# A hybrid decoder layer on one core: the edges of the first feed-forward reordered, and the mixer's output stage fed through another queue

## The chip, the core and the metric

The kernel runs on one core of one Trainium2 chip. The metric is device time in microseconds (us) of one execution. TensorE (PE in the profile) multiplies, VectorE (DVE), ScalarE (ACT) and GpSimd (POOL) compute on tiles, and SyncE (SP) only issues transfers. Transfers can be issued from SP, ACT and POOL; each of these works its own instructions off in order, so an issue that has to wait holds up all that stands behind it.

## The reference

One layer, sequence length 1024, model width 1024, all in float32:

```python
f = swiglu(rmsnorm(h, g1), w_gu, w_down)          # silu(h@Wg) * (h@Wu) @ Wd, d_ff = 2816
h = h + 0.5 * rmsnorm(f, g1_post)
m = hybrid_mixer(rmsnorm(h, g_mix), ...)          # 16 stick-breaking attention heads beside a
h = h + rmsnorm(m, g_mix_post)                    #   Mamba-2 scan; concat(att, ssd) @ w_out (2048 x 1024)
c = memory_cross_attention(rmsnorm(h, g_xa), rmsnorm(mem, g_mem), ...)
h = h + rmsnorm(c, g_xa_post)
f = swiglu(rmsnorm(h, g2), w_gu2, w_down2)        # the second feed-forward
return h + 0.5 * rmsnorm(f, g2_post)
```

Inside the mixer the attention output and the two groups of the scan's output each pass a norm of their own before `w_out`.

## The kernel before, in words

**Layout.** Activations lie transposed: 8 tiles `d` of 128 features, in two halves `hh` of 512 tokens. Every float32 operand is split into two float32r parts, hi (a rounded copy, made on ACT) and lo (the rest, made on DVE). A product is three matmuls: hi·hi, hi·lo and lo·hi (`mm3`). `XH[hh][d]` and `XL[hh][d]` are the two parts of the current input; `XH` tiles have one fixed place each, the `XL` tiles of a half share nine places (`xl0`, `xl1`) that go to whoever asks next.

**Order.** TensorE's order is written out by hand. `self.clock` adds up what each matmul is planned to cost (0.216 us for 512 columns), and a list `later` holds pieces of work for the other engines, each with a planned time; `run_later` issues what has come due, pinned behind what its engine was given before. `run_later(T)` takes all that is due up to T at once. Work that is not pinned is ordered by a planner with its own estimates.

**The first feed-forward, up (`up_phase`).** The first 3 of 22 blocks are plain products with weights split on the fly. The other 19 use Strassen-like sevens: seven products of quarter size (12 matmuls each) instead of eight (`seven`). A seven needs sums of input quarters: `S1`, `S4`, `S5`, and `B21`, `B12`, which overwrite the parts of the input that the plain products used. `fetch` reads the quarters a, d, b, c again from memory (pairs "ad", "bc"); `below` makes `B21` from the pair "ca" while the second half's plain products run, and `last` makes `B12` from the pair "bd" once they are done (`again` loads it). Each first scales one tile of its pair on ACT, then makes the difference on DVE and splits it. Two "ca" pairs lie in `raw2`, which is also where raw weights land; the other "ca" and the "bd" pairs lie in `blk` (three places, shared with split weights). The weights' own sums (`wc`) are made on GpSimd. For the blocks computed before block 4 the sums of activations that the down product needs are made from a copy read back from memory (`act_sums`, four loads on GpSimd's queue, five sums on DVE, five stores on ACT's queue); for the others `pair_sums` makes them from tiles still at hand. At its end `up_phase` calls `run_later(self.clock + 4600)`.

**Weights prepared ahead (`prepare`, `prepare_all`).** While the sevens run, 37 weights of the mixer's input product are loaded in 74 halves (256 KB), split, and both parts stored to memory, so that later they are only loaded. Loads and stores go on SP's queue; 62 halves have planned times 4.3 us apart, the last 12 fall in the down product, 9 us apart.

**Down (`down1`, `down7`).** Seven products `m` = 0 to 6, each over 11 blocks `j` of 256 features, 132 matmuls each. `fetch` loads for each j the weight and the sum of activations, on SP's queue; two of the four weight quarters stay in tiles named by `stay`, 11 each, in places of the former input. Weight and activation parts go to the eight places `wp` and `dx`, and to `hl`. After each product `finish` plans what follows: squares for the norm, loads of the residual (`resid`, GpSimd's queue), and `post`, which scales by the norm, adds the residual, stores the new h, and takes the columns and rows of the next norm (`rms_cols`, `rms_rows`: small products on TensorE) at two times named `tail`.

**Mixer.** `ssd` and `attention` follow. During `attention` 8 of the 16 weights of `w_out` (those of the scan's half) are prepared in 16 halves, 20 us apart; the other 8 are loaded raw and split when used. A head's output is added into `mix_d` in memory by accumulating transfers on GpSimd's queue (`finish`). `mix_first` does the first pass (half 0, scan part), six of eight output tiles beside the end of attention, the last two in `mix_out`. `mix_out` then does three passes: (half 0, attention), (half 1, scan), (half 1, attention), 192 matmuls each, two output tiles at a time. `load(kt, hh)` reads a tile of `mix_d` on SP's queue into `oraw` (four places), adds its square to a sum, and splits it. Weights come through `wstream`, one ahead, three places for hi and lo each; raw ones through two `wraw`.

Of the kernel before, what the change touches and what calls it, by code (L numbers as in the profile page):

```python
# [10 lines left out]
F32 = mybir.dt.float32  # L11
# [32 lines left out]

NOSYNC = mybir.DependencyInfo(mybir.DependencyClass.NoSync, mybir.DependencyReason.DATA)


class Kern:
# [142 lines left out]
    def prepare(self, names, raw, pairs, times):  # L191
# [9 lines left out]

        def load(n):
            pool, tag, bufs = raw[n % len(raw)]
            raws[n] = self.t(pool, [P, 4, P], F32, tag, bufs=bufs)
            self.kp(nc.sync.dma_start(out=raws[n], in_=work[n][0][:, work[n][2], :]))
# [9 lines left out]
        def store(n):  # L215
            for d, x in zip(work[n][1], parts.pop(n)):
                self.kp(nc.sync.dma_start(out=d[:, work[n][2], :].bitcast(F32), in_=x.bitcast(F32)))
# [20 lines left out]
    def prepare_all(self, sp):  # L238
# [9 lines left out]
        self.prepare(names, raw, pairs, a[:k] + [420000 + 9000 * i for i in range(n - k)])  # L248
# [124 lines left out]
    def resid(self, hh, step, start=0):  # L373


        def one(d):
            self.XL[hh][d] = self.xl(hh, F32)
            self.kp(self.nc.gpsimd.dma_start(out=self.XL[hh][d], in_=self.h[hh][d]))
# [179 lines left out]
    def up_phase(self, sp, sp2, wgu, gpre, act_d, bank, load, plain, sizes, rw=None, begin=None):  # L558
# [39 lines left out]
        def act_sums(j, t0):  # L598

            x = {}  # L600
            names = ("a11", "a21", "a12", "a22")

# [22 lines left out]
            for i, (n, out, a, b, op) in enumerate((  # L625
# [4 lines left out]
                at(t0 + 9000 + 1200 * i, combine, n, out, a, b, op)  # L630
                at(t0 + 12000 + 1200 * i, put, n)
# [29 lines left out]
        def tiles(n, src):  # L661
            if n in early:
                tmp[n] = self.t(rw, [P, 2, H], F32, "raw2", bufs=2)
            else:
                tmp[n] = self.t(sp2, [P, 2, H], F32, "blk", bufs=NBLK)
            for i, (hh, d) in enumerate(src):
                self.kp(nc.gpsimd.dma_start(out=tmp[n][:, i], in_=self.h[hh][d]))
# [21 lines left out]
        def steps(k):  # L689
            a, d = (lambda i=i: tmp["ad", k][:, i] for i in range(2))  # L690
            b, c = (lambda i=i: tmp["bc", k][:, i] for i in range(2))
# [12 lines left out]
        def below(k):  # L704
            c, a = (tmp["ca", k][:, i] for i in range(2))
            scale(a, k)
# [5 lines left out]
        def last(k):  # L712
            b, d = (tmp["bd", k][:, i] for i in range(2))
            scale(d, k + 4)
# [116 lines left out]
        early = [("ad", k) for k in range(4)] + [("ca", k) for k in range(2)] if begin else []  # L831
# [17 lines left out]
        if begin:  # L849
# [40 lines left out]
        for k in range(4):  # L890
# [23 lines left out]
    def down1(self, sp, wdn, act_d, xs_d, gpost, gnext):  # L914
# [4 lines left out]
        stay = {(1, 1): L_[0][4:8] + H_[0][4:8] + H_[0][0:3], (0, 0): H_[1][4:8] + L_[1][4:8] + H_[1][0:3]}  # L919
# [10 lines left out]
        def finish(m, i):  # L930
# [5 lines left out]
            elif m == 4:  # L936
# [968 lines left out]
    def mix_out(self):  # L1905
# [3 lines left out]
        with self.pools("mo", ["r", "a"], ["b"]) as (rp, sp, sp2, dnp):  # L1909
# [15 lines left out]
            def load(kt, hh):  # L1925
                raw = self.t(sp, [P, H], F32, "oraw", bufs=4)
                nc.sync.dma_start(out=raw, in_=self.mix_d[kt][:, hh * H : (hh + 1) * H])
                if kt < 8:
                    square(kt, raw)
# [5 lines left out]
                self.scaled_split(hi, lo, raw, self.par("ssd_norm_g" if kt >= 8 else "attn_norm_g", kt % 8))  # L1935
                return hi, lo
# [405 lines left out]
```

## Time and profile before

| what | us |
|---|---|
| median of 3 runs (lowest to highest) | 2640.93 (2639.95 to 2643.17) |
| the profiled execution: time, span | 2636.82, 2635.0 |
| PE busy, share of the span | 2586.5, 98% |
| DVE, ACT, POOL busy | 1983.5, 1292.7, 579.3 |
| mean clock granted to TensorE | 0.995 of full |
| up product of the first feed-forward ends at | 454 |
| attention and the first pass's start end at | 1576 |

The span runs from the first to the last instruction, and the rest of the time lies around it. In a row of a windows table "x" is the number of instructions in the stretch and PEclk the granted clock; a stretch of TensorE is undisturbed when 50 us hold 222 matmuls of 512 columns. A row of waits names who waited, on what, the total in us, how often, and the longest. A row of a timeline has start and length in us, engine, line, operation, tiles, and in brackets the idle time before it and what ended it; SPq and POOL rows with DMA are issues, whose data land later.

### The profile page before, as it was taken

Reading aid. Unit: us, or ns where it says so; the run is one execution under the profiler, and the core shown is the slowest. Engines: PE = TensorE matmul, PEld = TensorE weight load, DVE = VectorE, ACT = ScalarE, POOL = GpSimd, SP = SyncE. Lnnn points to the kernel's source line nnn. Section 1 sums busy time; section 2 is a strip of 40 time slices with the busy share of each in tenths; the row PEclk is TensorE's granted clock in tenths of the full one; section 3 lists DMA queues with packets and bytes.
Section 4 is the critical chain, followed back from the end, with each engine's and each line's share of the span. In section 5 each row is a group of like instructions: output and inputs, shape, how many; then the busy total and the mean of one; then the engine's idle time right before and its main releaser. Section 6 shows DMA issues by size and latency. Waiting matters only on the chain.

```text
span 2635.0 us, 36828 instructions
## 1 busy us (share of the span) xinstructions
PE 2586.5 (98%) x12850; PEld 2153.3 (82%) x12850; DVE 1983.5 (75%) x3044; ACT 1292.7 (49%) x2300; POOL 579.3 (22%) x677
## 2 busy tenths in 40 slices
PE   9999999999999999999999999999999999999999
PEld 7788887878777778888888897888878788888887
DVE  6778887779679774777777777767556888777777
ACT  7434443555356563555555555345554433333553
POOL 2555553000100000111111110101011555452000
PEclk9999999999999999999999999999999999999999
DMA  5558888884654226645555556547558453226654
GB/s 208 183 187 287 276 272 285 283 278 154 243 184 168 81 73 199 177 142 150 141 157 132 167 153 225 187 150 250 197 184 296 140 176 116 99 98 227 188 170 154
DMA packets 215274, 489.82 MB, mean 186 GB/s; under 512 B 26544, under 2 KB 35120, under 8 KB 215088
## 3 DMA queue, kind: packets, MB, share of 16 engines
q1 hardware_dynamic: 168656, 381.02, 44.1%
q0 software_dynamic: 23104, 63.98, 8.1%
q10 hardware_dynamic: 23328, 42.48, 4.3%
q8 instruction: 101, 1.65, 0.3%
q14 instruction: 85, 0.70, 0.1%
HBM read 327.46 MB, written 138.94 MB: 177 GB/s over the span
## 4 chain that ended last, share of the span: by engine, by line
PE 83%; DVE 6%; DMA 5%; issue 3%; ACT 2%; POOL 1%; SPq 0%; DVEq 0%; POOLq 0%; ACTq 0%
PE mm L139 45%; PE dn L139 30%; PE z L139 2%; PE tr L142 2%; PE y L139 1%; PE ms L142 1%; PE ms L139 1%; DMA wraw<-in_w_dn 1%; PE seg L139 1%; DMA oraw<-mix 1%; DVE nb L1731 1%; DVE wlo L265 1%; PE st L139 0%; POOL wc L732 0%; DMA ev<-mix 0%
## 5 line engine op out<-in xcount | busy, mean ns | idle before, releaser
L139 PE MATMUL mm<-xh,whi 128*128 128x512 f32 x1320 | 520.5, 403 | 5.3 <-DVE xl L1899 2.3
L139 PE MATMUL mm<-xh,wlo 128*128 128x512 f32 x1272 | 489.1, 392 | 0.6 <-ACT xh L263 0.6
L139 PE MATMUL mm<-xl,whi 128*128 128x512 f32 (+1 forms) x1252 | 486.7, 389 | 1.5 <-DVE xl L265 1.2
L139 PEld LDWEIGHTS mm<-xh,whi 128*128 128x128 f32 x1320 | 248.3, 188 | 47.3 <-issue 3.8
L139 PEld LDWEIGHTS mm<-xh,wlo 128*128 128x128 f32 x1272 | 238.9, 188 | 53.0 <-ACT xh L263 1.0
L139 PEld LDWEIGHTS mm<-xl,whi 128*128 128x128 f32 x1252 | 236.2, 189 | 35.1 <-DVE xl L265 1.6
L1731 DVE TENSOR_TENSOR_SCAN nb<-nb,begin 128x128 f32<-128x128 f32 (+7 forms) x128 | 171.5, 1352 | 52.3 <-ACT nb L1727 51.4
L1727 ACT ACTIVATE nb<-z,scale 128x128 f32<-128x128 f32 (+2 forms) x192 | 107.9, 581 | 77.3 <-PE z L139 76.9
L265 DVE TENSOR_TENSOR wlo<-wraw,whi 128x1024 fp32r<-128x1024 f32 x70 | 85.4, 1221 | 54.2 <-ACT whi L263 53.9
L263 ACT CAST whi<-wraw 128x1024 fp32r<-128x1024 f32 (+1 forms) x87 | 83.8, 964 | 78.6 <-PE mm L139 54.2
L654 ACT ACTIVATE ft<-ft 128x512 f32<-128x512 f32 x88 | 55.5, 632 | 106.6 <-DVE ft L653 104.7
L1748 POOL DMA_DIRECT2D mix<-sq x64 | 52.8, 826 | 228.2 <-DVE sq L1746 168.2
L139 PE MATMUL dn<-xh,wlo 128*128 128x512 f32 x296 | 101.2, 390 | 1.3 <-DMA wlo<-dwlo 1.3
L732 POOL TENSOR_TENSOR wc<-wraw,raw 128x512 f32<-128x512 f32 x56 | 79.5, 1420 | 60.7 <-DVE whi L265 16.0
L732 POOL TENSOR_TENSOR wc<-raw,wraw 128x512 f32<-128x512 f32 x55 | 81.6, 1484 | 50.7 <-DVE blk L265 21.3
L265 DVE TENSOR_TENSOR atl<-tr,ath 128x512 fp32r<-128x512 f32 (+1 forms) x108 | 67.9, 631 | 29.9 <-ACT ath L263 29.6
L817 POOL TENSOR_TENSOR ft<-ft,e 128x512 f32<-128x512 f32 x37 | 60.0, 1622 | 121.2 <-DVE e L816 45.0
L263 ACT CAST ath<-tr 128x512 fp32r<-128x512 f32 (+1 forms) x108 | 58.9, 546 | 55.2 <-PE tr L142 50.9
L139 PE MATMUL mm<-ath,v 128*128 128x256 f32 x320 | 85.7, 290 | 0.3
L139 PE MATMUL dn<-xh,blk 128*128 128x512 f32 x264 | 85.2, 389 | 0.0
L263 ACT CAST wlo<-wc 128x512 fp32r<-128x512 f32 x79 | 49.1, 621 | 70.7 <-PE dn L139 23.7
L139 PE MATMUL mm<-atl,v 128*128 128x256 f32 x320 | 82.7, 281 | 0.7 <-DVE atl L265 0.7
(552 smaller groups left out, 6777.2 us busy)
## 6 DMA issues: line engine op xcount, KB each, us to landing
whi<-dwhi SPq DMA_DIRECT2D x82, 512.0 KB, 3.6
wlo<-dwlo SPq DMA_DIRECT2D x82, 512.0 KB, 4.7
wraw<-in_w_gu SPq DMA_DIRECT2D x43, 512.0 KB, 4.0
raw<-in_w_gu SPq DMA_DIRECT2D x37, 512.0 KB, 4.2
dwhi<-bh SPq DMA_DIRECT2D x70, 256.0 KB, 4.1
dwlo<-bl SPq DMA_DIRECT2D x70, 256.0 KB, 4.2
wraw<-xs SPq DMA_DIRECT2D x56, 256.0 KB, 3.1
xs<-ft ACTq DMA_DIRECT2D x54, 256.0 KB, 3.1
```

The lines of the kernel that those rows point to most:

```text
L139: self._pe(self.nc.tensor.matmul(out, lhsT, rhs, start=start, stop=stop, skip_group_check=self.more), cost)
L142: self._pe(self.nc.tensor.transpose(out, src, self.ident if ident is None else ident), 109.0)
L263: self.kp(self.nc.scalar.copy(hi, src))
L265: self.nc.vector.tensor_tensor(out=lo, in0=src, in1=hi.bitcast(F32), op=ALU.subtract)
L654: nc.scalar.activation(t, t, AF.Silu)
L732: nc.gpsimd.tensor_tensor(out=t, in0=a, in1=b, op=op)
L817: nc.gpsimd.tensor_tensor(out=t1, in0=t1, in1=e, op=ALU.mult)
L1727: nc.scalar.activation(nb[:, s0:s1], z[:, 0:n], AF.Sigmoid, scale=sc[:, i : i + 1])
L1731: nc.vector.tensor_tensor_scan(out=nb[:, 0:Wd][:, ::-1], data0=nb[:, 0:Wd][:, ::-1], data1=begin[:, S - Wd : S][:, ::-1], initial=0.0, op0 ...
L1748: nc.gpsimd.dma_start(out=self.mix_d[p][a * 64 : a * 64 + 64, csl], in_=o, accum_op=ALU.add)
```

## The change

Eight things change in the first feed-forward, and three in the mixer. The second feed-forward shares `up_phase` and keeps its path (`begin` is None there).

1. Three of the "ca" pairs and three of the "bd" pairs get places of their own (`homes`: `braw` twice, `rpost` and `dg`, `acc0` and `acc1`, which the preparation of weights uses only later); none lies in `raw2` any more, and of these pairs `blk` holds two instead of six. The first three "ca" loads are planned 13, 18.5 and 5 us earlier, the first three "bd" loads 9.5, 7 and 4.5 us earlier.
2. The scaling of a tile of the pair is taken out of `below` and `last` and planned on its own, before them.
3. `last` is planned every 1.2 us instead of 1.5.
4. `act_sums` makes its sums 14 us after its loads are planned instead of 9, and stores 3 us after that.
5. The call `run_later(self.clock + 4600)` at the end of `up_phase` is gone.
6. In `down1` the stay tiles of quarter (1, 1) are taken in another order: the first four are `XH[0][4:8]`, the next four `XL[0][4:8]`.
7. The last 12 halves of prepared weights are loaded and stored on GpSimd's queue (`switch`).
8. The columns and rows of the next norm of half 0 are planned at 17 and 20.5 us after the last tile instead of 11 and 16, and the first four squares of half 1 15 us later and closer together.
9. All 16 weights of `w_out` are prepared during attention, 32 halves, 12 us apart.
10. `mix_out` reads attention's tiles back on GpSimd's queue, into eight places of `oraw`, the eight of its first pass in one go, and squares them after the split.
11. The residual's loads in `mix_out` start later (16 us, then 3.5 us apart) and each waits for the TensorE instruction that was last issued when it was planned (`hold`).

```diff
-    def prepare(self, names, raw, pairs, times):
+    def prepare(self, names, raw, pairs, times, switch=float("inf")):
+        def queue(n):
+            return nc.sync if times[n] < switch else nc.gpsimd
...
-        self.prepare(names, raw, pairs, a[:k] + [420000 + 9000 * i for i in range(n - k)])
+        self.prepare(names, raw, pairs, a[:k] + [420000 + 9000 * i for i in range(n - k)], 418000)
...
+    def hold(self, inst):
+        self.tc.add_manual_dep(inst.ins, self.prev.name, SYNC, reason="not before this product")
...
+            late = 14000 if begin else 9000
-                at(t0 + 9000 + 1200 * i, combine, n, out, a, b, op)
-                at(t0 + 12000 + 1200 * i, put, n)
+                at(t0 + late + 1200 * i, combine, n, out, a, b, op)
+                at(t0 + late + 3000 + 1200 * i, put, n)
...
-        early = [("ad", k) for k in range(4)] + [("ca", k) for k in range(2)] if begin else []
+        early = [("ad", k) for k in range(4)] if begin else []
+        homes = {}
+        if begin:
+            for k, x in enumerate((
+                [(rw, "braw", 2)] * 2, [(rw, "rpost"), (self.tp, "dg")], [(rw, "acc0"), (rw, "acc1")],
+            )):
+                homes["ca", k] = homes["bd", k] = x
...
-            for k, t in enumerate((27000, 33500, 34000, 34500)):
+            for k, t in enumerate((14000, 15000, 29000, 34500)):
                 at(t0 + t, tiles, ("ca", k), [(0, k + 4), (0, k)])
+                at(t0 + 34000 + 1500 * k, lambda k=k: scale(tmp["ca", k][1], k))
...
-                            at(self.clock + 12500 + 500 * k, again, k)
+                            at(self.clock + 3000 + 3000 * k, again, k)
+                            at(self.clock + 12000 + 1000 * k, lambda k=k: scale(tmp["bd", k][1], k + 4))
...
-            at(self.clock + 1500 * k + (0 if begin else 500), last, k)
+                at(self.clock + 3500, lambda: scale(tmp["bd", 3][1], 7))
+            at(self.clock + (1200 * k if begin else 1500 * k + 500), last, k)
...
-        self.run_later(self.clock + 4600)
+        if not begin:
+            self.run_later(self.clock + 4600)
...
-        stay = {(1, 1): L_[0][4:8] + H_[0][4:8] + H_[0][0:3], (0, 0): H_[1][4:8] + L_[1][4:8] + H_[1][0:3]}
+        stay = {(1, 1): H_[0][4:8] + L_[0][4:8] + H_[0][0:3], (0, 0): H_[1][4:8] + L_[1][4:8] + H_[1][0:3]}
...
-                self.post(0, gpost, self.C[0], gnext, step=2600, accs=accs[:])
+                self.post(0, gpost, self.C[0], gnext, step=2600, accs=accs[:], tail=(17000, 20500))
-                    at(2000 + 4000 * d, squares, 1, d, "bh")
+                    at(17000 + 2500 * d, squares, 1, d, "bh")
...
-            self.prepare([("out", i) for i in range(8, 16)], *self.prep_pool(wsp), [self.clock + 30000 + 20000 * i for i in range(16)])
+            self.prepare([("out", i) for i in [*range(8, 16), *range(8)]], *self.prep_pool(wsp), [self.clock + 30000 + 12000 * i for i in range(32)])
...
+            def read(kt, hh):
+                raw = self.t(sp, [P, H], F32, "oraw", bufs=8)
+                nc.gpsimd.dma_start(out=raw, in_=self.mix_d[kt][:, hh * H : (hh + 1) * H])
+                return raw
...
-            for k in range(8):
-                prefetch(1, k)
-            self.resid(0, 5000, 12000)
+            raws = [read(k, 0) for k in range(8)]
+            acts[1] = [load(k, 0, raws[k]) for k in range(8)]
+            self.resid(0, 3500, 16000, True)
```

More of the change, by code (lines that the diff above doesn't have):

```diff
@@ L662, in tiles @@
             if n in early:
-                tmp[n] = self.t(rw, [P, 2, H], F32, "raw2", bufs=2)
-            else:
-                tmp[n] = self.t(sp2, [P, 2, H], F32, "blk", bufs=NBLK)
-            for i, (hh, d) in enumerate(src):
-                self.kp(nc.gpsimd.dma_start(out=tmp[n][:, i], in_=self.h[hh][d]))
+                t = self.t(rw, [P, 2, H], F32, "raw2", bufs=2)
+            elif n in homes:
+                t = [self.t(*x[0:1], [P, H], F32, *x[1:]) for x in homes[n]]
+            else:
+                t = self.t(sp2, [P, 2, H], F32, "blk", bufs=NBLK)
+            tmp[n] = t if isinstance(t, list) else [t[:, i] for i in range(2)]
+            for x, (hh, d) in zip(tmp[n], src):
+                self.kp(nc.gpsimd.dma_start(out=x, in_=self.h[hh][d]))
         def scale(x, d):
@@ L712, in last @@
         def last(k):
-            b, d = (tmp["bd", k][:, i] for i in range(2))
-            scale(d, k + 4)
+            b, d = tmp["bd", k]
+            if not begin:
+                scale(d, k + 4)
             combine(B12[k], b, k, d, ALU.subtract)
@@ L1923, in square, with load @@
                     nc.vector.tensor_tensor(out=asum[-1], in0=asum[-1], in1=sq, op=ALU.add)
[L1925 to L1929, printed above, removed]
+            def read(kt, hh):
+                raw = self.t(sp, [P, H], F32, "oraw", bufs=8)
+                nc.gpsimd.dma_start(out=raw, in_=self.mix_d[kt][:, hh * H : (hh + 1) * H])
+                return raw
+            def load(kt, hh, raw=None):
+                if raw is None:
+                    raw = read(kt, hh)
                 if kt < 8:
```

23 lines of the change are left out of this document (15 added, 8 removed).

## The prediction, made before the change was run

> **What bounds the kernel now.** I read the page first, then the waits of TensorE, then windows around each wait, then the timelines of the engines that caused it.
>
> ```profile
> span 2635.0 us, 36828 instructions
> PE 2586.5 (98%) x12850; PEld 2153.3 (82%) x12850; DVE 1983.5 (75%) x3044; ACT 1292.7 (49%) x2300; POOL 579.3 (22%) x677
> ```
>
> TensorE is the bound. No part of the change takes a matmul away, so all that can be won is time in which TensorE waits or runs at a lower clock. These are the waits in the stages that the change touches (who <- on what: us, times, longest).
>
> ```profile
> PE dn L139 <- ACT whi L998: 6.5, 1, 6.5
> PE mm L139 <- DVE xl L265: 2.6, 3, 1.2
> PE ms L139 <- DVE acc L365: 2.5, 2, 2.3
> PE mm L139 <- ACT xh L263: 2.4, 2, 1.8
> PE dn L139 <- ACT F L1050: 1.6, 1, 1.6
> PE dn L139 <- DVE olo L272: 1.5, 2, 0.8
> PE dn L139 <- DMA wlo<-dwlo: 1.3, 1, 1.3
> PE dn L139 <- DVE e L796: 0.8, 1, 0.8
> PE mm L139 <- DVE e L796: 0.7, 1, 0.7
> ```
>
> The last two rows are those of the stretch 75 to 150. A wait costs more than its length where the clock falls after it. The windows show it (us, PE busy with number of matmuls, the other engines, PEclk, DMA share, GB/s):
>
> ```profile
> 88.08:91.50 3.42, 3.42 (x9) 2.65 (x10) 2.95 (x5) 2.44 (x5) 1.46 (x3) 0.50 0.88 286
> 101.73:105.15 3.42, 3.42 (x10) 2.64 (x9) 3.42 (x6) 0.62 (x1) 2.19 (x2) 0.50 0.00 0
> 456.72:463.55 6.83, 3.22 (x8) 2.43 (x9) 5.80 (x9) 4.02 (x7) 1.32 (x3) 0.50 1.01 350
> 668.35:671.76 3.41, 3.41 (x10) 2.63 (x9) 3.41 (x7) 1.24 (x2) 0.54 (x1) 0.50 1.03 409
> 1596.77:1600.19 3.42, 3.38 (x8) 2.48 (x8) 3.42 (x5) 2.09 (x4) 0.00 (x0) 0.50 0.46 159
> 200.00:250.00 50.00, 50.00 (x222) 41.40 (x222) 42.42 (x61) 23.11 (x41) 28.24 (x19) 1.00 0.82 281
> 50.00:100.00 50.00, 46.20 (x193) 36.70 (x191) 40.66 (x53) 28.15 (x47) 23.87 (x32) 0.97 0.60 205
> 100.00:150.00 50.00, 47.32 (x200) 38.28 (x200) 35.41 (x52) 15.79 (x28) 30.76 (x27) 0.97 0.50 175
> 450.00:500.00 50.00, 43.53 (x186) 35.47 (x185) 40.96 (x66) 29.11 (x52) 3.19 (x4) 0.93 0.91 319
> ```
>
> 222 matmuls in 50 us make 0.225 us each and 15.2 in 3.42 us. So the five dips cost (15.2-9), (15.2-10), (14.3-8, in the 3.22 us that were busy), (15.2-10) and (15.2-8) matmuls: 1.4, 1.2, 1.4, 1.2 and 1.6 us. The counts bound the stages: 50 to 150 lacks 222-193 + 222-200 = 51 matmuls or 11.5 us, 450 to 500 lacks 36 or 8.1 us.
>
> **The change, part by part.**
>
> *Start of the sevens (homes, scaling apart, earlier loads).* Size: 2.6 + 2.4 of waits and 1.4 + 1.2 of dips, 7.6 us. What lies behind them, on GpSimd:
>
> ```profile
> 63.29 1.06 POOL L667 DMA_DIRECT2D raw<-in_xT  x2 [1.78 <-ACT S L263]
> 69.99 1.06 POOL L667 DMA_DIRECT2D raw<-in_xT  x2 [5.64 <-issue]
> 90.03 1.06 POOL L667 DMA_DIRECT2D blk<-in_xT  x2 [2.15 <-DVE bl L683]
> ```
>
> The "ca" pairs wait at 63 and 70 for `raw2` to be given up, and the last "bd" pair at 90 for `blk`. These places are the cause: the change gives the pairs others, empty until 152 of the planner's time. No instruction is added; four ACT scalings move ahead, still before their readers. The loads move past GpSimd's sums of weights, which at POOL's 24 to 31 us per 50 have room. B12 can only be written after the last plain product, and its fourth pair is still in `blk`: this may leave a rest. Bounds 0 and 10 (11.5 less the next 1.5). I take 7.
>
> *act_sums 5 us later.*
>
> ```profile
> 115.52 5.17 DMA dg<-act
> 120.16 1.29 DVE L616 TENSOR_TENSOR xl<-cb,cb 128x512 f32<-128x512 f32 x2 [3.93 <-DMA cb<-act]
> ```
>
> DVE stood 3.9 us for data that landed at about 120; 5 us later they are there. What DVE held up was e, for which TensorE waited 0.8 and 0.7. Now `cb`'s three places come free 5 us later, and `pair_sums` of block 5 needs them: DVE could stand there instead. Bounds -3.9 and 1.5; I take 1.4, as the planner knows that order.
>
> *Edge to the down product (stay order, no `run_later`, GpSimd's queue).*
>
> ```profile
> 435.54 5.32 SPq L984 DMA_DIRECT2D xh<-in_w_dn  x8
> 454.68 3.17 SPq L984 DMA_DIRECT2D xl<-in_w_dn  x4
> SPq L217 <- DVE bl L213: 3.0, 2, 1.9
> 454.68 4.95 DMA xl<-in_w_dn
> ```
>
> The first two are from SP's timeline, the third from its waits between 425 and 470, the last from the chain that ended last. The first down product starts with the stay tiles in `xl`, issued last, at 454.7, when the last seven's B11 frees them; the `xh` ones were issued at 435. With `xh` first, the four blocks that are needed first are there by 454. The `xl` ones are then needed from 454 + 4 x 2.7 = 465, and landed by about 463 (issued to 457.9, 4.95 to land), with their split still to come: little slack, so a rest may come back. Without `run_later` SP does not meet the stores of prepared halves that are due then before the first seven fetches; the activation stores that go later with them are read four blocks on, 10 us. Size: 6.5 + 1.4 = 7.9 (count: 8.1). Bounds 0 and 8.1; I take 6.8.
>
> [...] The sum above rests on the order of the stay tiles.
>
> Those halves cost GpSimd 36 issues at about 0.54 us each (the 1.06 of two above), 19 us on an engine that is busy 3.2 of 50 us there; SP no longer stands for their conversions. What this is worth is the wait for F, 1.6: bounds 0 and 1.6, I take 0.8.
>
> *Norm of half 0 later, squares of half 1 later.* The 2.3 us wait for acc and its dip, 3.5 together, go if DVE is done six us later; the four squares that made way for it run beside the last product, 30 us long, and nobody reads them before its end. The rows are then planned 35.8 + 20.5 = 56.3 us after `post`, and the two products left last 264 x 0.216 = 57.0: they just fit. Bounds 1.2 (the 2.3 wait returns at the end) and 3.5; I take 3.
>
> *Attention: 16 more halves.*
>
> ```profile
> 1025.00:1575.00 550.00, 542.66 (x3183) 472.07 (x3182) 399.67 (x560) 295.77 (x598) 75.25 (x192) 1.00 0.55 154
> L213 DVE TENSOR_TENSOR bl<-braw,bh x16: 667/681/693, 1059.6 to 1380.2; 128x512 fp32r<-128x512 f32 x16
> ```
>
> Each adds a DVE instruction of 0.68, an ACT one like it, one load and two stores on SP. DVE has 150 us free of 550. In the tile's query nobody waited for the sixteen that are there. Bounds 0 and 16 x 0.68 = 10.9; I take 0.5.
>
> *mix_out.*
>
> ```profile
> 1575.56 2.27 SPq L1927 DMA_DIRECT2D oraw<-mix  x4
> 1583.52 3.88 SPq L1927 DMA_DIRECT2D oraw<-mix  x4
> 1632.00:1677.00 45.00, 43.72 (x205) 35.61 (x204) 31.56 (x49) 14.46 (x24) 4.31 (x8) 1.00 0.63 217
> 1677.00:1722.00 45.00, 45.00 (x211) 37.44 (x210) 34.92 (x53) 18.47 (x28) 4.30 (x8) 1.00 0.44 146
> 1661.07 7.09 DMA wlo<-dwlo
> xl<-h POOLq DMA_DIRECT2D x16, 256.0 KB, 4.9
> oraw<-mix SPq DMA_DIRECT2D x24, 256.0 KB, 4.3
> wlo<-dwlo SPq DMA_DIRECT2D x8, 512.0 KB, 5.0
> ```
>
> (The last three are issues between 1575 and 1722.) The second four reads waited for places until 1583.5; with eight places all go together, and the residual's eight, which ran among them, are held back. The residual's last issue is then planned at 16 + 7 x 3.5 = 40.5 and its first reader 45 + 14 = 59, so the pass of 45 us hides it; were one late, DVE would stand for the 4.9 us of its landing. Gain: olo 1.5 and 0.9 of the dip (the rest is the second wait itself) and 0.6 for ca: 3.0; I take 2, bounds 0 and 3.
>
> Against it: two passes now load weights as hi and lo. The pass 1632 to 1677, which did, held 205 matmuls, the raw one after it 211: 6 x 0.225 = 1.35 us, twice 2.7. The cause is that the second weight of a pair gets its place after 36 of the pair's 48 matmuls and is needed after 60, 24 x 0.225 = 5.4 us for a landing of 5.0 + 0.4 of issue. Bounds 0 and the second rival's 26; I take 2.7. The 16 splits of raw weights that are saved there stood beside products (DVE is busy 35 of 45 us in the raw pass): nothing.
>
> Sum: 7 + 1.4 + 6.8 + 0.8 + 3 + 2 = 21.0, less 0.5 + 2.7: 17.8 us. The profiled execution took 2636.8 and would take 2619.0; the median of the runs is 4.1 above it, so I forecast 2640.9 - 17.8 = 2623.
>
> **Rivals.**
>
> *The relief comes back downstream.* For: the DMA share at the edge; TensorE only meets earlier what lands no sooner. Against: fetches are paced by places that TensorE frees, not by time. With start 4, sums 1.4, edge 2, F 0, norm 2, mix_out 1, less 3.2: 7.2 won, 2634.
>
> *Slower: the weights of mix_out come too late.* Landing as at 1661, 7.1 + 0.4 against 5.4, every pair loses 2.1 us and a dip of 1.2: 3.3 x 8 = 26.4 instead of 2.7, or 2647. It decides from 21.0/8 = 2.6 us per pair on. For: eight residual loads still run beside the first of these passes, eight stores and loads beside the second. Against: it befell one pair of four in the pass that has them.
>
> [...]
>
> *All waits go and nothing is paid:* 7.6 + 1.5 + 7.9 + 1.6 + 3.5 + 3.0 + 1.3 = 26.4, 2614.5.
>
> **How the numbers follow.** Forecast (2617 to 2630) 0.47, all won 0.14, back downstream 0.20, reads late 0.04, slower 0.15. A change of 0.2% is 5.3 us; the three runs lie within 0.12%. Faster: 0.47 + 0.14 + 0.04 + 0.13 of the downstream case = 0.78; same: its other 0.07 and 0.01 of the slower case; slower 0.14. The range 2608 to 2638 leaves out the slower case and the far end of the downstream one. The forecast alone is 2617 to 2630.
>
> **What would show it.** Right: no wait for whi L998 over 1 us, 450 to 500 at 215 matmuls or more, clock 1.00 at 88, 102, 457 and 668; "ca" loads issued before 60 us; 98 loads whi<-dwhi instead of 82, and 32 braw<-in_w_out instead of 16. Wrong: waits for wlo<-dwlo or whi<-dwhi of 2 us and more between 1587 and 1722, a new wait of DVE for `cb` near 150, or new waits for hl or whi between 460 and 600.

## The result, and the profile after

| | median of the runs, us (lowest to highest) | the profiled execution, us (span) |
|---|---|---|
| before, measured beside | 2640.05 (2634.88 to 2643.66) | 2636.82 (2635.0) |
| changed | 2640.53 (2635.23 to 2645.91) | 2645.91 (2643.8) |

The ratio is 1.0006 (95% interval 0.9998 to 1.0015): no difference that can be measured, where 2623 was forecast. The profile of the changed kernel is of its longest run and the one of before is of a short run, so of the 8.8 us between the two traces most is the execution and not the change. What the change did must be read place by place.

From the page of the changed kernel (span, busy times):

```profile
span 2643.8 us, 36945 instructions
PE 2590.8 (98%) x12850; PEld 2155.5 (82%) x12850; DVE 1973.2 (75%) x3044; ACT 1284.2 (49%) x2300; POOL 612.6 (23%) x737
```

The waits of TensorE in the changed kernel (who, on what: us, times, longest):

```profile
PE dn L140 <- ACT F L1077: 5.4, 1, 5.4
PE dn L140 <- DMA wlo<-dwlo: 4.4, 5, 1.4
PE mm L140 <- DVE xl L269: 4.2, 3, 1.7
PE dn L140 <- ACT F L1072: 3.1, 1, 3.1
PE mm L140 <- ACT xh L267: 2.7, 2, 1.6
PE dn L140 <- DMA whi<-dwhi: 2.3, 2, 1.9
PE dn L140 <- DVE e L813: 0.8, 1, 0.8
PE dn L140 <- DVE hl L269: 0.7, 1, 0.7
PE dn L140 <- ACT dx L267: 0.5, 1, 0.5
```

The wait of 6.5 us for whi at 457, the waits for acc, for olo and one of the two for e are gone. New are waits for F of 5.4 us (at 555) and 3.1 (at 488), for hl and dx (at 670), and seven waits for prepared weights in `mix_out` instead of one. The waits for xl and xh that were at 86 are at 92 to 102 now, and all of them together are longer (6.9 us, before 5.0). The windows of the same kernel, with the places of before first and the new ones after them:

```profile
85.50:88.90 3.40, 3.40 (x17) 2.82 (x16) 0.42 (x1) 2.73 (x6) 0.00 (x0) 1.00 0.67 234
453.60:460.40 6.80, 6.80 (x32) 5.63 (x31) 4.49 (x9) 3.66 (x7) 2.34 (x3) 1.00 0.99 351
96.31:106.55 10.24, 6.63 (x13) 4.00 (x14) 10.24 (x13) 4.03 (x7) 5.98 (x5) 0.50 0.18 67
488.84:492.25 3.41, 3.41 (x10) 2.47 (x9) 3.41 (x7) 3.41 (x8) 0.00 (x0) 0.50 0.43 131
553.69:560.52 6.83, 5.29 (x13) 4.14 (x14) 6.31 (x11) 4.74 (x9) 1.60 (x3) 0.50 0.52 182
673.16:676.57 3.41, 3.41 (x8) 2.44 (x8) 2.43 (x5) 0.63 (x1) 0.00 (x0) 0.50 1.01 392
50.00:100.00 50.00, 44.49 (x190) 35.47 (x189) 38.66 (x50) 27.11 (x45) 27.32 (x33) 0.96 0.60 200
100.00:150.00 50.00, 47.69 (x198) 38.12 (x197) 35.16 (x53) 16.13 (x28) 27.91 (x25) 0.93 0.50 169
450.00:500.00 50.00, 46.95 (x201) 38.16 (x200) 41.09 (x67) 29.14 (x53) 7.95 (x14) 0.97 0.88 308
550.00:600.00 50.00, 44.77 (x186) 36.81 (x187) 36.37 (x59) 25.46 (x47) 9.60 (x18) 0.93 0.74 245
```

The clock is full at 86 and 457, where it was halved before. But it is halved for 10.2 us from 96 on, 50 to 150 holds 388 matmuls where it held 393, and 550 to 600 holds 186; the same stretch before held 213:

```profile
550.00:600.00 50.00, 48.35 (x213) 39.53 (x212) 38.20 (x62) 28.35 (x52) 2.15 (x4) 1.00 0.76 242
```

### The profile page after: what moved, and what is told of

It is laid out like the page before. It is cut to its first block, busy times and chain, and to the rows that moved or that the text cites. A ratio compares the mean times of both kernels' runs of the same rounds, so it can differ in the third digit from the quotient of the medians.

```text
span 2643.8 us, 36945 instructions
## 1 busy us (share of the span) xinstructions
PE 2590.8 (98%) x12850; PEld 2155.5 (82%) x12850; DVE 1973.2 (75%) x3044; ACT 1284.2 (49%) x2300; POOL 612.6 (23%) x737
## 5 line engine op out<-in xcount | busy, mean ns | idle before, releaser
L269 DVE TENSOR_TENSOR wlo<-wraw,whi 128x1024 fp32r<-128x1024 f32 x54 | 65.9, 1221 | 52.6 <-ACT whi L267 49.2
L267 ACT CAST whi<-wraw 128x1024 fp32r<-128x1024 f32 (+1 forms) x71 | 67.2, 946 | 72.1 <-PE mm L140 55.0
L267 ACT CAST whi<-wc 128x512 fp32r<-128x512 f32 x80 | 49.7, 621 | 70.5 <-PE dn L140 25.9
L140 PE MATMUL dn<-xh,whi 128*128 128x512 f32 x240 | 83.2, 392 | 0.1
```

Source lines behind the costliest of these rows:

```text
L140: self._pe(self.nc.tensor.matmul(out, lhsT, rhs, start=start, stop=stop, skip_group_check=self.more), cost)
L267: self.kp(self.nc.scalar.copy(hi, src))
L269: self.nc.vector.tensor_tensor(out=lo, in0=src, in1=hi.bitcast(F32), op=ALU.subtract)
```

## The experiments

**One table for all.** TensorE does the same 12850 matmuls in nearly the same order in all these kernels, so the start of the n-th one can be compared. A column is a stretch, named by its times in the kernel before; a number is by how many us the kernel became later (+) or earlier (-) in it, against the trace of before. In a stretch outside these a kernel differs by at most 2.7 us, with both signs; all of them together make -1.5 to +4.2 us.

| kernel | 19-118 start of the sevens | 118-152 sums | 447-473 edge | 473-523 | 523-593 | 637-696 norm | 1572-1700 mix_out | span |
|---|---|---|---|---|---|---|---|---|
| changed | +2.2 | -0.9 | -8.3 | +5.0 | +6.1 | +0.1 | +2.9 | 2643.8 |
| stay order alone | -0.4 | -0.3 | -8.3 | +7.2 | +0.9 | -0.9 | +0.3 | 2636.5 |
| stay order, no call | +1.6 | +0.1 | -8.3 | +1.9 | +2.8 | -0.2 | +0.9 | 2636.6 |
| halves on SP | +2.8 | -1.8 | -8.3 | +1.3 | +1.9 | -1.2 | +1.6 | 2632.3 |
| no late stores | +0.7 | -1.4 | -8.3 | +5.7 | -2.1 | -0.9 | +1.7 | 2630.6 |
| their loads on SP | +3.0 | -1.7 | -8.3 | +2.5 | +6.0 | -0.9 | -0.5 | 2636.6 |
| scale in last | +0.3 | -1.3 | -8.3 | +6.5 | +4.3 | -0.2 | +1.5 | 2640.0 |
| eight w_out | +2.9 | -1.5 | -8.3 | +3.8 | +5.7 | 0.0 | -4.5 | 2634.3 |
| three undone | +1.6 | -1.2 | -8.3 | +2.2 | +1.4 | -0.2 | -0.7 | 2629.7 |
| three undone, again | +0.5 | -1.8 | -8.3 | +1.5 | -0.5 | -1.1 | -1.8 | 2627.5 |
| and no hold | +0.4 | -2.0 | -8.3 | +2.6 | +0.1 | -0.8 | -2.8 | 2624.4 |
| and no hold, again | -0.7 | -1.5 | -8.3 | +1.9 | +4.0 | +0.3 | -3.7 | 2628.7 |
| no hold, old start | +3.2 | -0.3 | -8.3 | +2.8 | +3.5 | -0.2 | -3.6 | 2632.7 |
| no hold, old norm | -1.4 | -1.6 | -8.3 | +1.9 | +1.1 | -0.1 | -3.8 | 2623.8 |
| no hold, old norm, again | +0.6 | -1.6 | -8.3 | +2.8 | +2.4 | -0.3 | -1.1 | 2633.7 |
| no hold, reads on SP | +1.1 | -1.3 | -8.3 | +2.4 | +3.4 | -1.1 | -2.1 | 2627.7 |

Rows that share the code of a column show how far one execution scatters: -0.4 to +3.2 in the first column for the three with the old start, -0.5 to +4.0 in 523-593 for those with the halves on SP's queue. So means are used below.

### The edge, and what came back behind it

The stay order alone, on the kernel before:

```diff
-        stay = {(1, 1): L_[0][4:8] + H_[0][4:8] + H_[0][0:3], (0, 0): H_[1][4:8] + L_[1][4:8] + H_[1][0:3]}
+        stay = {(1, 1): H_[0][4:8] + L_[0][4:8] + H_[0][0:3], (0, 0): H_[1][4:8] + L_[1][4:8] + H_[1][0:3]}
```

> The kernel before with the new order of the stay tiles alone. Theory (the order takes the wait at 457 away, and the same loads are then late at 488 and 555 because the data land no sooner): 5 to 8 us are won by 470 us and at least 4 of them are lost by 600; total 0 to 4 us less than before. Rival (what was lost downstream came from the other edits, the halves on GpSimd's queue and the call left out): at least 5 us of the gain are still there at 600, total 5 to 8 us less. Third: the order alone wins less than 2 us, because SP first meets the stores of prepared halves.

It won 8.3 us at the edge, the whole of the wait and its dip, and lost 7.2 at 488 and 0.9 at 557: all of it. Ratio 0.9990 (0.9979 to 1.0001). In this kernel ScalarE's timeline (start, length, operation, idle time before it and what ended it) shows what is late at 488:

```profile
477.82 0.62 ACT L263 CAST hl<-raw 128x512 fp32r<-128x512 f32 x1 [1.63 <-DMA raw<-xs]
479.92 0.62 ACT L263 CAST hl<-wraw 128x512 fp32r<-128x512 f32 x1 [1.48 <-DMA wraw<-xs]
483.99 0.62 ACT L263 CAST hl<-raw 128x512 fp32r<-128x512 f32 x1 [1.20 <-DMA raw<-xs]
488.40 1.56 ACT L1045 ACTIVATE F<-dn 128x512 f32<-128x512 f32 x3
```

ScalarE stands in its order for activation sums that have not landed, and the copy of the finished product, F, which TensorE needs to have its bank back, comes behind them. TensorE used to stand at 457, and these loads had that time; now they have not. Next, the call left out as well:

```diff
-        self.run_later(self.clock + 4600)
         return xs_d
```

> The kernel before with the new order of the stay tiles and without the call of run_later at the end of the up product; nothing else. With the order alone 8.2 us were won at 457 and 7.2 lost at 488, 0.9 at 557; in the changed kernel with its halves on SP's queue the losses were 1.3 and 1.9. Theory (the call puts work that is due up to 4.6 us later, ScalarE's stores and SP's, ahead of the down product's first loads, and so delays them): without it the loss at 488 falls to 1 to 3 us. Rival (it was another edit of the changed kernel, or chance in the order of transfers): the loss at 488 stays at 5 us or more.

The loss at 488 fell from 7.2 to 1.9, and 1.9 of that came back at 557. So the call costs 3 to 5 us beside the new stay order, by one trace of each kernel; what it costs with the old order was not run. Then the changed kernel with its 12 halves back on SP's queue:

```diff
-        self.prepare(names, raw, pairs, a[:k] + [420000 + 9000 * i for i in range(n - k)], 418000)
+        self.prepare(names, raw, pairs, a[:k] + [420000 + 9000 * i for i in range(n - k)])
```

> The changed kernel, but the last 12 prepared halves go on SP's queue again. The changed kernel won 8.3 us at the edge (454 to 462) and lost 5.0 at 488 and 6.1 at 555. Theory (on GpSimd's queue the halves' loads and stores no longer wait their turn among the down product's loads, come in groups of three 256 KB transfers, and slow these loads): the wait of 5.4 us at 555 falls to 2 or less, 4 us come back there; the loss at 488 changes by less than 2. Rival (what was won at the edge comes back because the DMA engines are full, whichever queue issues): both losses stay within 1.5 us.

Ratio 0.9980 (0.9971 to 0.9990). At 555 the theory held. At 488 it did not: 3.7 us came back there too. Over the kernels made from the changed one, the loss in 473-523 is 5.3 on the mean where GpSimd issues these loads, 2.2 where all halves are on SP's queue; in 523-593 it is 5.5 where GpSimd issues the stores, 1.9 with all on SP's. Two runs part these. The first leaves out the late stores, so that its output is another; it is read for its times alone. The second gives the loads alone back to SP's queue:

```diff
-            for d, x in zip(work[n][1], parts.pop(n)):
+            for d, x in zip(work[n][1], parts.pop(n) if times[n] < switch else parts.pop(n)[:0]):
```

> The changed kernel, its last 12 halves on GpSimd's queue as they are, but their 24 stores of 256 KB are left out, and the products that would read them read the parts of the six weights before them (so the output is another). To be read only between 450 and 700 us, where the changed kernel lost 5.0 at 488 and 6.1 at 557 against the kernel before, and the same kernel with these halves on SP's queue 1.3 and 1.9. Theory (the bytes are the cost: the DMA engines are full and each of these transfers delays a load that a product waits for): with 6.3 MB less the losses fall to 1.5 or less each. Rival (the order is the cost: the loads of these halves come from GpSimd ahead of what SP has to issue, and their conversions stand in ScalarE's and VectorE's order): the losses stay above 3 us each.

```diff
-            self.kp(queue(n).dma_start(out=raws[n], in_=work[n][0][:, work[n][2], :]))
+            self.kp(nc.sync.dma_start(out=raws[n], in_=work[n][0][:, work[n][2], :]))
```

> The changed kernel, the loads of the last 12 halves on SP's queue and their stores still on GpSimd's. To be read between 450 and 600. With both on GpSimd's queue 5.0 us were lost at 488 and 6.1 at 555, without the stores 5.7 and -2.1, with both on SP's 1.3 and 1.9. Theory (at 488 the loads are the cost: from GpSimd they come ahead of what SP has waiting; at 555 the stores are): the loss at 488 falls to 2.5 or less, that at 555 stays at 4 or more. Rival (any transfer that does not take its turn on SP's queue costs at both): both stay at 4 or more. Third (the loads are the cost at both): both fall below 3.

Without the stores the loss at 488 stayed (5.7) and the one at 555 turned into a gain of 2.1; with the loads on SP's queue the one at 488 fell to 2.5 and the one at 555 stayed (6.0). So the two places have two causes: at 488 the loads, at 555 the stores.

At 488 the loads cost by the order of ScalarE's instructions. Here is ScalarE in the changed kernel, and then in one made from it with its halves on SP's queue (three parts undone, below):

```profile
482.60 0.62 ACT L267 CAST hl<-raw 128x512 fp32r<-128x512 f32 x1 [2.02 <-DMA raw<-xs]
483.13 0.62 ACT L267 CAST whi<-cb 128x512 fp32r<-128x512 f32 x1
487.36 0.59 ACT L1072 ACTIVATE F<-dn 128x512 f32<-128x512 f32 x1
```

```profile
480.31 0.62 ACT L267 CAST whi<-cb 128x512 fp32r<-128x512 f32 x1
481.97 0.62 ACT L267 CAST hl<-raw 128x512 fp32r<-128x512 f32 x1 [1.04 <-DMA raw<-xs]
485.00 0.59 ACT L1069 ACTIVATE F<-dn 128x512 f32<-128x512 f32 x1
```

With the loads on GpSimd's queue, the copy `hl` that stands for an activation sum comes ahead of the weight's copy `whi`; VectorE then stands 2.4 us for `whi`, and F comes later. From the start of that `hl` to F it is 4.8 us in all four kernels whose loads GpSimd issues, and 3.0 to 3.2 in all ten that are made from the changed one with these loads on SP's queue. These 1.7 us are over half of the 3.1 between the means. A piece of halved clock follows in three of the four and in none of the ten. The activation sums themselves land hardly later (between 466 and 490 after 4.8 us, with the halves on SP's queue after 4.5 to 4.7).

VectorE's timeline of the changed kernel shows the cause at 555:

```profile
550.25 0.69 DVE L1020 TENSOR_TENSOR cb<-wraw,xl 128x512 f32<-128x512 f32 x1 [3.01 <-DMA wraw<-in_w_dn]
553.87 0.69 DVE L1042 TENSOR_TENSOR ft<-dn,F 128x512 f32<-128x512 f32 x1
```

VectorE stands 3.0 us for a weight quarter, and `add` for the finished product, on which F and then TensorE wait, is behind it. The transfers between 530 and 552 (KB each, median us from issue to landing), first in the changed kernel, then without the late stores:

```profile
wraw<-in_w_dn SPq DMA_DIRECT2D x3, 256.0 KB, 5.7
wraw<-xs SPq DMA_DIRECT2D x3, 256.0 KB, 6.0
dwhi<-acc POOLq DMA_DIRECT2D x1, 256.0 KB, 6.4
```

```profile
wraw<-in_w_dn SPq DMA_DIRECT2D x4, 256.0 KB, 2.9
wraw<-xs SPq DMA_DIRECT2D x4, 256.0 KB, 3.2
```

A load that takes 2.9 us takes 5.7 with GpSimd's stores around it. The bytes alone are not the reason: with all halves on SP's queue as many move in these 22 us (5.95 MB, against 5.75 in the changed kernel), and the load takes

```profile
wraw<-in_w_dn SPq DMA_DIRECT2D x3, 256.0 KB, 3.9
```

In the changed kernel GpSimd issues a store, a load and a store from 542.35 to 543.95, and the load for which VectorE stands at 550.25 is issued at 544.43, right behind them. With the halves on SP's queue the transfers next to that load are issued at 536.88, 537.25 and 546.00, and it at 539.29. Whether they would cost the same from ScalarE's queue was not run.

### The start of the sevens

```diff
         def last(k):
             b, d = tmp["bd", k]
-            if not begin:
-                scale(d, k + 4)
+            scale(d, k + 4)
...
-                            at(self.clock + 12000 + 1000 * k, lambda k=k: scale(tmp["bd", k][1], k + 4))
...
-                at(self.clock + 3500, lambda: scale(tmp["bd", 3][1], 7))
```

> The changed kernel, but the scaling of the 'bd' tiles is done inside last again; the 'ca' scalings stay apart. In the changed kernel ScalarE stood 3.5 us at 85 us for a 'bd' tile, behind it stood the weight splits, and TensorE lost 5.7 us against the kernel before between 92 and 104 us. Theory (a scaling planned ahead is a place in ScalarE's order, and it parks the engine): that stand is gone, the loss of 5.7 us shrinks to 2 or less, total about 4 us less than the changed kernel. Rival (VectorE is full there beside GpSimd's sums, with instructions of 1.75 us, whatever ScalarE does): less than 1.5 us of the 5.7 comes back.

In the changed kernel ScalarE and VectorE stood like this:

```profile
85.30 0.72 ACT L685 ACTIVATE dg<-dg,params 128x512 f32<-128x512 f32 x1 [3.50 <-DMA dg<-in_xT]
87.83 0.61 ACT L267 CAST whi<-wraw 128x512 fp32r<-128x512 f32 x1
88.48 0.69 DVE L269 TENSOR_TENSOR whi<-wraw,whi 128x512 fp32r<-128x512 f32 x1 [5.17 <-ACT whi L267]
```

That stand is gone with the scaling back in `last`. Over all kernels the first column is +2.3 on the mean where the scalings are planned ahead, +0.3 where they are in `last`: 2 us, half of what was expected; the total did not move measurably (ratio 1.0002, 0.9992 to 1.0012). Of the 4.4 us that are won by 92, 4.2 are still lost by 104; counted in this way (by the same matmuls as in the table) the changed kernel loses 6.8 there. So 2.6 us came back, more than the rival's 1.5 and less than the theory asks for: both have a part. VectorE and GpSimd there, scale in `last`:

```profile
94.14 1.76 DVE L698 SCALAR_TENSOR_TENSOR bl<-acc,params,acc 128x512 f32<-128x512 f32 x1
95.83 0.74 DVE L698 SCALAR_TENSOR_TENSOR bh<-blk,params 128x512 f32<-128x512 f32 x1
97.69 1.76 DVE L269 TENSOR_TENSOR wlo<-wc,wlo 128x512 fp32r<-128x512 f32 x1
```

```profile
94.06 1.30 POOL L807 TENSOR_TENSOR sq<-sq,sq 128x512 f32<-128x512 f32 x1 [0.39 <-ACT sq L806]
97.24 1.67 POOL L748 TENSOR_TENSOR wc<-raw,wraw 128x512 f32<-128x512 f32 x1 [1.89 <-DVE whi L269]
```

VectorE has no idle time of 0.3 us from 89 to 104, and in these rows the two instructions that begin while one of GpSimd runs (at 94.14 and 97.69) take 1.76 us each. The scaling and difference at 95.83, while GpSimd stands, takes 0.74, and the next `wlo<-wc`, at 103.07 with GpSimd standing again, takes 0.68. The control, with the old start:

```diff
-                homes["ca", k] = homes["bd", k] = x
...
-            for k, t in enumerate((14000, 15000, 29000, 34500)):
+            for k, t in enumerate((27000, 33500, 34000, 34500)):
...
-                            at(self.clock + 3000 + 3000 * k, again, k)
+                            at(self.clock + 12500 + 500 * k, again, k)
```

> The kernel without the hold (three parts undone, residual planned as before), and with the start of the sevens as in the kernel before as well: the 'ca' and 'bd' pairs in their old places, loaded and scaled at the old times; the sums of act_sums stay 5 us later. Theory (the places were not the limit: VectorE is full from 85 to 105 us, so what is won at 86 is lost at 92 to 101): at 125 us the kernel is within 1.5 us of the one without the hold, after the first 40 us are set off. Rival (the prediction's reading, the loads were late): 4 us or more are lost by 125 us.

From 29 to 125 us it lost 2.3 us: more than the theory's 1.5, less than the rival's 4. (At 118 it was 1.4; the rest is the wait at 123 that is told below.) Near 90 it was 7.2 us later, and 6.0 of that came back by 107. On the means the old start has +1.1 (four traces, the one of before among them), the new one 0.3 with the scaling in `last`: the places and the early loads are worth 0.8 us, within the scatter. Ratio of this kernel 0.9965 (0.9950 to 0.9981), against 0.9964 with the new start (without the hold, below): no difference. That VectorE's backlog is the limit there is read from the traces; nothing was run that takes work from it.

The same run says something of `act_sums`, of which no run of its own was made. VectorE's stand for the loaded sums is shown in the prediction, 3.93 us before 120.16. In the changed kernel it reads

```profile
120.86 1.29 DVE L628 TENSOR_TENSOR xl<-cb,cb 128x512 f32<-128x512 f32 x2 [4.23 <-DMA cb<-act]
```

The first sums are at the same place in VectorE's order, and VectorE stands for them as long as before. What is won between 118 and 152 is 1.0 us at 123, alike in all 13 kernels with the new start, and 0.2 to 1.0 at 143 in twelve of them (with the old start 0 to 0.4). The kernel with the old start and the later sums wins nothing at 123, like the three with the old sums. So at 123 the gain comes with the new start and not with the later sums; what in the new start does it was not traced.

### The output stage of the mixer

```diff
-            self.prepare([("out", i) for i in [*range(8, 16), *range(8)]], *self.prep_pool(wsp), [self.clock + 30000 + 12000 * i for i in range(32)])
+            self.prepare([("out", i) for i in range(8, 16)], *self.prep_pool(wsp), [self.clock + 30000 + 20000 * i for i in range(16)])
```

> The changed kernel, but only the eight w_out weights of the scan's half are prepared, 20 us apart as before; the reads on GpSimd's queue, the eight places and the held residual stay. Theory (hi and lo weights of 1 MB a pair arrive too late in mix_out): the waits for wlo<-dwlo and whi<-dwhi, 6.7 us together, fall to 2 or less between 1576 and 1722, where the changed kernel lost 2.8 us against the kernel before, and the stage ends 3 to 4 us earlier. Rival (the weights are late because the residual's and the tiles' reads fill the DMA engines): raw weights are late too or their splits are, and the stage ends less than 1.5 us earlier.

Ratio 0.9986 (0.9977 to 0.9996). The waits for prepared weights fell from 6.7 to 0.3 us, as the theory has it; a wait of 1.4 for the split of a raw weight came. Over all kernels `mix_out` is at +1.4 with 16 prepared weights, at -2.3 with eight (residual held): 3.7 us. The transfers between 1580 and 1612 of the changed kernel:

```profile
oraw<-mix POOLq DMA_DIRECT2D x24, 256.0 KB, 5.7
whi<-dwhi SPq DMA_DIRECT2D x4, 512.0 KB, 8.1
wlo<-dwlo SPq DMA_DIRECT2D x4, 512.0 KB, 9.8
```

The weights' parts land after 8.1 and 9.8 us beside 24 reads. Now the three costly parts undone at once (the diffs for the halves, the scaling and the w_out weights, together):

> The changed kernel with the three parts undone that the runs before this one showed to cost time: the 'bd' scalings in last again, the last 12 halves on SP's queue, eight w_out weights prepared instead of 16. Theory (the three costs are separate places and add): against the changed kernel's profiled execution 1 to 2 us less at 104 us, about 9 less between 480 and 680, 6 to 8 less between 1590 and 1690; the span is 2625 to 2629 instead of 2643.8, and the time 0.3 to 0.5 percent below the kernel before. Rival (what is won at one place comes back at the next): the span is 2631 to 2635, like that of the single steps, and the time at most 0.2 percent below the kernel before.

Median 2629.10, ratio 0.9962 (0.9949 to 0.9974): faster than the kernel before, and by the ratios (the changed kernel 1.0006) than the changed one. The three do add within the interval: one at a time they took 0.0004, 0.0026 and 0.0020 off the changed kernel's ratio, which makes 0.9956 together. At the three places of the traces it is 0.6, 7.5 and 3.6 us better than the changed kernel; 1 to 2, 9 and 6 to 8 were expected, so each is smaller, and the span is 14.1 us shorter, just short of the 15 to 19 of the theory. The hold and the queue of the reads, on this kernel:

```diff
-            self.resid(0, 3500, 16000, True)
+            self.resid(0, 5000, 12000)
```

> The kernel of the first of these four runs, but the residual's loads in mix_out are planned as in the kernel before (12 us, then 5 us apart) and not held to a product. Theory (the early residual loads took DMA time from the reads of attention's tiles, and that made olo late): waits for olo of 1 to 2 us and a dip of the clock come back at 1594 to 1600, 2 to 3 us in all. Rival (the eight places were what helped): less than 0.7 us is lost there.

```diff
-                nc.gpsimd.dma_start(out=raw, in_=self.mix_d[kt][:, hh * H : (hh + 1) * H])
+                nc.sync.dma_start(out=raw, in_=self.mix_d[kt][:, hh * H : (hh + 1) * H])
```

> The kernel without the hold, and with the reads of attention's tiles on SP's queue, still into eight places. Theory (SP stands in this stretch for stores of the attention's state, and a read behind them is late): waits for olo come back at 1580 to 1595, 1.5 to 4 us. Rival (eight places are what took the waits away, whichever queue issues): less than 0.7 us of waits for olo, and the stage from 1565 to 1680 within 1 us.

Neither brought the waits for olo back. The waits of `mix_out` without the hold, and then with the reads on SP's queue too:

```profile
PE dn L140 <- DVE wlo L269: 1.8, 1, 1.8
PE dn L140 <- DMA wlo<-dwlo: 1.1, 1, 1.1
```

```profile
PE dn L140 <- DVE wlo L269: 2.2, 1, 2.2
PE dn L140 <- DMA wlo<-dwlo: 1.1, 1, 1.1
PE ms L140 <- DVE asum L1947: 0.4, 1, 0.4
```

So neither the queue nor the hold took the olo waits away. What is left are the eight places, with the reads in one go and the squares after the split; no run brings the four places back or parts these three. With eight prepared weights the stretch is 2.7 us (residual held) to 3.4 us (not held) better on the means than with the old output stage. That the kernel without the hold had a trace 5.3 us shorter asked for a comparison side by side, with the norm's old times as a third:

> The changed kernel with the three costly parts undone ('bd' scalings in last, halves on SP's queue, eight w_out weights), residual held: timed again beside the two that follow. Its one profile was 5.3 us longer than that of the kernel without the hold, though only 2 us of it lie in mix_out, where one had a drop of the clock and the other none. Theory (the 5.3 us were chance: which waits cost a drop of the clock differs from execution to execution): over several runs its median lies within 2.6 us (0.1 percent) of the next kernel's. Rival (the hold costs time): it is slower by 3.5 us or more.

> The same kernel with the residual planned as in the kernel before and not held. Theory: median 2626 to 2632, ratio to the kernel before 0.995 to 0.997, within 2.6 us of the kernel with the hold. Rival: 3.5 us or more below it.

Medians 2630.99 with the hold and 2631.40 without; ratios to before 0.9967 (0.9955 to 0.9979) and 0.9964 (0.9951 to 0.9977). Over several runs the 5.3 us are not there: they were chance, as the theory has it.

### The norm

```diff
-                self.post(0, gpost, self.C[0], gnext, step=2600, accs=accs[:], tail=(17000, 20500))
+                self.post(0, gpost, self.C[0], gnext, step=2600, accs=accs[:])
...
-                    at(17000 + 2500 * d, squares, 1, d, "bh")
+                    at(2000 + 4000 * d, squares, 1, d, "bh")
```

> The kernel without the hold, and with the norm of half 0 and the squares of half 1 planned as in the kernel before. Theory (VectorE has a backlog at 655 to 668, and the wait only moves from acc to hl and dx): the wait for acc of 1.8 to 2.3 us comes back, the waits for hl and dx at 658 to 666 go, and between 640 and 690 us the kernel loses 0 to 1.5 us. Rival (the prediction's 3 us): it loses 2.5 us or more there.

> The kernel without the hold, and with the norm of half 0 and the squares of half 1 at their old times. Theory (VectorE's backlog only moves the wait): median within 2.6 us of the kernel without the hold and with the new times. Rival (the prediction's 3 us): 2.7 us or more above it.

The wait for acc (2.2 us) came back, those for hl and dx went, and between 640 and 690 the first of the two lost 0.7 us. Timed, the kernel with the old times has 2631.19, against 2631.40 with the new. On the means the norm's stretch is 0.2 us better with the new times.

## Why the prediction was wrong

- **Edge: right in size at its place, wrong downstream.** The order of the stay tiles alone gave the whole 8.3, where 6.8 was taken. "A rest may come back" was costed at 1.1; 4.1 comes back at 488 and 557 in the best case, 8.1 with the call in place, 10.8 with GpSimd's halves. The loads behind the four blocks were the ones without slack, and ScalarE's order passes that on to F. The rival that the relief comes back downstream had the mechanism.
- **Wait for F, 0.8 won by GpSimd's queue: the wrong sign.** The prediction let the bound end at 0 on the other side and had no term for what else the queue decides. The move cost 6.7 us: 3.1 at 488 by the loads, most of it by a changed order on ScalarE, and 3.6 at 555 by the stores, which go out right ahead of a load that VectorE needs. The DMA share of 450 to 500 is 0.88 (before 0.91), so the trace shows hardly more room there. At 555 the load that VectorE needs takes 5.7 us in the changed kernel, and 3.9 with as many bytes (5.95 MB against 5.75) on SP's queue.
- **Start of the sevens, 7 of 7.6: about -1.2, within the scatter of single traces; timed, no difference.** Two steps failed. The four scalings were costed at nothing because they come "still before their readers"; their cover was the landing of the pair, and when that was late they held up the weight splits: 2 us. And the waits at 86 were put down to places alone; by the traces VectorE is full to 104, and B12 takes back what B21 wins (not shown by a run).
- **act_sums, 1.4: the number by luck, the step failed.** The stretch is 1.4 better on the means and one of the two waits for e is gone. But by the prediction the data are there when the sums come 5 us later, and VectorE stands 4.2 us for them, where it stood 3.9; the kernel that keeps the later sums without the new start wins 0.3 in the whole stretch. No new wait for `cb` came.
- **Norm, 3 of 3.5: 0.2.** The wait for acc goes, and hl and dx wait instead. VectorE's backlog before 668 (no idle time from 652 on, before the change) was not asked for.
- **Attention's 16 halves, 0.5: not to be told from nothing.** Between 1030 and 1572 the five kernels with 32 halves are 1.2 us later on the mean than the trace of before, the others 0.2, and single ones -1.3 to +2.7. The loads are 98 whi<-dwhi and 32 braw<-in_w_out, as said.
- **mix_out: gain 2, cost 2.7, measured 2.7 to 3.4 and 3.7.** Both near in size. The slower rival's mechanism is there, but a wait is 0.2 to 1.9 us and not 3.3, below the 2.6 per pair from which it decides. Late reads, which the prediction gives a chance of 0.04, are shown by no run: the reads issued between 1574 and 1590 land after 5.9 us in the median on GpSimd's queue, and after 5.9 on SP's before the change.

The sum with these sizes is -1.2 + 1.4 + 8.3 - 5.3 - 5.5 + 0.2 - 1.0 = -3.1: a loss of 3.1 us where 17.8 were to be won. Between the medians the loss is 0.5 (by the interval -0.5 to +4.0), so the sum agrees within the noise and not more closely. The steps that failed most are the start of the sevens (7 taken, nothing won) and the edge with GpSimd's queue (6.8 + 0.8 taken, 2.5 lost).

## What to carry to other kernels

A wait that is taken away is only won if the loads for the next two stages have slack without it: look behind it for the next instruction that stands in its engine's order for a transfer, and count that as late by the whole gain. Moving transfers to another queue changes more than who issues them: here they came right ahead of a load that others needed, and the order of another engine's instructions changed with them, so compare the order on each engine before and after. A later time in a plan is not a later place in an engine's order: look at the trace before an effect is put down to it. Work planned ahead takes a place in an engine's order, and costs nothing only while its own input is certain to be there.

## What the runs showed of the hardware

The halved clock comes in pieces of 3.41 us (3.41, 6.83 and 10.24 in the clock records of the kernel before and the changed one). In each of these two traces they begin whole multiples of 3.41 us apart (before, 88.08 and 101.73: four; changed, 96.31 and 488.84: 115). The same wait brings one in some traces and none in others. The wait for sq near 1010 to 1020 lasts 1.9 to 2.2 us in all 17 traces, and a piece of 3.41 us follows in 13 of them. The window around it with a drop (three undone) and without (no hold):

```profile
1009.30:1015.90 6.60, 4.67 (x27) 4.50 (x26) 2.89 (x7) 0.98 (x3) 0.94 (x1) 0.74 0.64 238
```

```profile
1005.00:1011.00 6.00, 4.06 (x34) 3.89 (x34) 4.86 (x8) 2.39 (x4) 0.94 (x1) 1.00 0.45 166
```

In the kernel before a wait of 3.2 us at 2100 brought none; it did in the 16 others. So a wait of 1.9 us can be enough for a piece, and one of 3.2 us can pass without. Several such places, each worth 1.2 to 1.6 us like the five dips counted in the prediction, explain a good part of the spread between the runs of one kernel: the 31 runs of the kernel before beside the first four experiments lie within 9.4 us, their mean clock between 0.991 and 0.995, and 0.001 less goes with 1.8 us more (correlation -0.72, or half of the variance). So one trace is not enough for a difference of 0.2%.
